# Gate columns of the modulation: both blocks of a tile behind its second half

## The chip, the cores and the metric

The kernel runs on one core of one Trainium2 chip. The metric is the device time of one execution in microseconds (us), taken as the median of several runs. PE is the TensorE engine (matmuls), PEld its weight loads, DVE is VectorE, ACT is ScalarE, POOL is GpSimd, SP is SyncE, whose queue issues the loads.

## What is computed

One step of a hybrid decoder layer for 1024 prompt tokens and 8 sampled sequences of 8 tokens, model width 2048. Cut to what matters here:

```
mod = silu(c) @ w_ada + b_ada            # c: one prompt row and 8 sample rows
shift, scale, gate = split(mod, 3)
xn  = rmsnorm(x, norm_g) * (1 + scale) + shift
z   = xn @ w_in                          # 40 tiles of 128 columns, cut into 8 parts
...                                      # three token mixers: RG-LRU, convolution, spatial gating
out = concat(ya, yb, yc) @ w_out
y   = rmsnorm(x + gate * out, final_g)
```

`shift` and `scale` are needed before `xn`, `gate` only when the out-projection is read out. So the 2048 columns of `w_ada` that give `gate` can be multiplied at any time before that.

## The kernel before

Everything is float32. A large matmul is made of three float32r products: each operand is split into a high and a low part (`split`: a copy on ACT gives the high part, a subtraction on DVE the low part), and `mm3` (L135) adds hi·hi, hi·lo and lo·hi. Those three are the lines L136, L137 and L138 of every table.

The tokens go through in two parts: first 512 prompt tokens (T0), then the other 512 and the 64 sample tokens (T1). The first part begins with the 4096 columns of shift and scale (`ada_block`, tile a_raw), interleaved with six in-projection tiles (`k_step`). Then `IN_SINGLE` lists 34 in-projection tiles of 128 columns, n = 0 to 33, which the loop at L760 does one after the other.

One such tile is `single` (L541). Its weights come in two halves, `h` = 0 and 1, each a load of 512 KB (`w_raw`, three buffers) that is split into two pieces `w_hi`, `w_lo` (five and four buffers). Each half is 8 k-steps of three matmuls, so 24 matmuls of 128x512, all into one PSUM tile `ps_s`. Behind each half `single` calls `extra(h)`.

For the last 16 tiles, n = 18 to 33, `extra` multiplies gate columns. `gate_block` (L156) does one block f of 32: it takes two buffers `g_raw` (the pool tag xr, four buffers), loads 256 KB of `w_ada` into each, and calls `ada_mm` (L147), which issues 8 matmuls of the modulation rows `cz` (32 columns wide, so each fills a quarter of the array's columns) against 128 columns; in the profile a block is 16 matmuls at L151 into `ps_ada`. Eight blocks fill one `ps_ada`; behind the last of them `ada_fin` copies it (ACT, tile rows), transposes it (PE, L174) and adds the bias (DVE, adam).

`ps_s`, `ps_ada` and the out-projection's `ps_g` share three PSUM buffers (pool pmm). While a `ps_ada` is open, the tiles use the other two.

A scheduler sets the order on each engine. It takes the instructions in the order of the program; what stands under `high_priority` (the loads of `w_raw` and `g_raw` and the splits) is taken as if it stood some thousand places earlier, as far as its buffer is free by then. SP issues its loads in that order, and one that waits for its buffer holds up those behind it.

Behind a tile, `part.step()` runs what was deferred by a tile (the gates of the RG-LRU group, `ps_gate`, L440, six pairs of matmuls with 64 rows), and `part.finish` reads the tile out of PSUM, for the RG-LRU tiles with an ACT copy into `pad_a` (L419).

Of the kernel before, what the change touches and what calls it, by code (L numbers as in the profile page):

```python
# [44 lines left out]
def decoder_layer(ctx: ExitStack, tc: tile.TileContext, a):  # L45
# [101 lines left out]
    def ada_mm(pa, b, raw):  # L147
        for q in range(2):
            k = 2 * b + q
            for j in range(4):  # L150
                nc.tensor.matmul(pa[32 * j:32 * j + 32, 0:P], cz[:, k, :], raw[q][:, j * P:(j + 1) * P],  # L151
                                 start=(k == 0), stop=(k == KT - 1))
# [3 lines left out]
    def gate_block(f):  # L156
        u, b = 8 + f // 8, f % 8
        if b == 0:
            gate_ps[u] = pmm.tile([P, 2, 512], F32, tag="mm", name="ps_ada")[:, 0, :]
        raw = []  # L160
        with tc.high_priority(HP):
            for q in range(2):
                r = sp_.tile([P, TM], F32, tag="xr", name="g_raw")
                nc.sync.dma_start(r[:, :512], a["w_ada"][u, b][:, q * 512:(q + 1) * 512])
                raw.append(r)
        ada_mm(gate_ps[u], b, raw)
        if b == 7:
            ada_fin(u, gate_ps[u])

    def ada_fin(u, pa):  # L170
        rows = stp.tile([P, P], F32, tag="rows", name="rows", bufs=1)
        with tc.high_priority(HP):
            nc.scalar.copy(rows, pa[:, 0:P])
        nc.tensor.transpose(pa[:, P:2 * P], rows, ident)  # L174
        with tc.high_priority(HP):
            dst = adam[:, 4 * u:4 * u + 4, :]
            o = VEC["b_ada"][0] + 4 * u
            nc.vector.tensor_tensor(dst, pa[:, P:2 * P].rearrange("p (a b) -> p a b", b=32)[:, :, 0:9],
                                    vec[:, o:o + 4].unsqueeze(2).to_broadcast([P, 4, 9]), op=ALU.add)
            if u < 8:  # L180
                o = VEC["norm_g"][0] + 2 * u
                sc = dst.rearrange("p (a b) n -> p a b n", b=2)[:, :, 1, :]
                nc.vector.scalar_tensor_tensor(
                    sc, sc, 1.0, vec[:, o:o + 2].unsqueeze(2).to_broadcast([P, 2, 9]),
                    op0=ALU.add, op1=ALU.mult)
# [355 lines left out]
    def single(src, xs, T, extra=None):  # L541
        ps = pmm.tile([P, 2, 512], F32, tag="mm", name="ps_s")
        for h in range(2):
            hl = load_w(src[h], 1024, 2)
            for kk in range(8):
                k = h * 8 + kk
                xh, xl = xs(k)
                hi, lo = hl[kk // 4]
                o = kk % 4 * P
                mm_unit(ps, 0, hi[:, o:o + P], lo[:, o:o + P], xh, xl, T,  # L550
                        k == 0, k == KT - 1)
            if extra:
                extra(h)
        return ps
# [205 lines left out]
    for n, ct in enumerate(IN_SINGLE):  # L760
        g0 = (n - 18) * 2
        ps = single(a["wi_s"][n], lambda k: xn[k], T0,
                    (lambda h: gate_block(g0 + h)) if g0 >= 0 else None)
        part.step()
        part.finish(ct, ps, 0)
    part.step(True)
# [119 lines left out]
```

## Time and profile before

| | us |
|---|---|
| median of 3 runs | 1499.89 |
| lowest and highest of these | 1499.72, 1502.18 |
| the profiled execution, its own time | 1500.81 |
| its span, from the first to the last instruction | 1499.1 |
| PE busy in the span | 1457.4 |

The profile is of one execution. The table of all engines says who is busy, the list of waits who stood still and for whom, a timeline shows the starts of the instructions one by one. Matmuls are pipelined: the time one of them takes on the engine is the distance from its start to the next start, not its listed duration, which is longer. A window row gives the busy time of each engine in a stretch, the number of instructions, and the granted TensorE clock as a share of full speed.

### The profile page before, as it was taken

To read this page: it belongs to the slowest core of one execution; us is meant where nothing else is said; L and a number is where in the kernel's file an instruction comes from. 1 tells how busy PE (TensorE), PEld (TensorE's weight loads), DVE (VectorE), ACT (ScalarE), POOL (GpSimd) and SP (SyncE) were. 2 spreads that over 40 slices of the span, in tenths; PEclk is the share of its full clock that TensorE was granted. 3 is DMA by queue.
4 is the path that set the end of the run, shared out by engine and by line. 5 is a ranking of instruction groups with operands and counts; after the bars stand their busy time and mean duration, and the time that the engine had idled before them with its cause. 6 is when DMAs were issued, how large, how long until landed. Compare 5 with 4: busy or idle time off the path is not lost.

```text
span 1499.1 us, 25363 instructions
## 1 busy us (share of the span) xinstructions
PE 1457.4 (97%) x10108; PEld 1304.8 (87%) x10108; DVE 902.0 (60%) x1708; ACT 622.0 (41%) x1042; POOL 49.8 (3%) x120
## 2 busy tenths in 40 slices
PE   4999999999999999999999999999999999999996
PEld 3777888887777778888899999999999999999996
DVE  4436983679467452554895993388956755334345
ACT  4224432274557542443533422236455854223220
POOL 0000000000000000000000100011000000000000
PEclk9999999999999999999999999999999999999998
DMA  9995233324554542564473222222222221244323
GB/s 365 407 361 196 82 102 98 98 91 145 162 162 143 168 152 99 176 196 151 151 246 110 83 86 76 83 85 88 88 87 71 71 89 55 80 130 124 109 79 127
DMA packets 86550, 205.05 MB, mean 137 GB/s; under 512 B 10656, under 2 KB 26656, under 8 KB 86432
## 3 DMA queue, kind: packets, MB, share of 16 engines
q1 hardware_dynamic: 85280, 202.25, 40.8%
q8 instruction: 79, 1.29, 0.3%
q10 hardware_dynamic: 1152, 1.18, 0.2%
q14 instruction: 39, 0.32, 0.1%
HBM read 193.65 MB, written 9.74 MB: 136 GB/s over the span
## 4 chain that ended last, share of the span: by engine, by line
PE 91%; DMA 6%; DVE 2%; issue 0%; ACT 0%; SPq 0%; DVEq 0%; ACTq 0%
PE ps_s L136 24%; PE ps_s L138 23%; PE ps_s L137 23%; PE ps_g L138 5%; PE ps_g L136 5%; PE ps_g L137 5%; DMA a_raw<-w_ada 5%; PE ps_ada L151 2%; PE ps_gate L440 1%; DMA w_raw<-wi_g 1%; DMA x<-x 1%; PE ps_bc L206 1%; PE ps_mix L333 1%; DVE y L643 0%; PE ps_var L215 0%
## 5 line engine op out<-in xcount | busy, mean ns | idle before, releaser
L98 DVE TENSOR_TENSOR w_lo<-w_raw,w_hi 128x512 fp32r<-128x512 f32 (+1 forms) x480 | 311.5, 653 | 408.7 <-PE ps_s L138 264.5
L136 PE MATMUL ps_s<-xn_hi,w_hi 128*128 128x288 f32 (+1 forms) x1632 | 540.6, 331 | 1.8 <-ACT pad_a L419 1.6
L97 ACT CAST w_hi<-w_raw 128x512 fp32r<-128x512 f32 (+1 forms) x480 | 281.1, 591 | 611.4 <-PE ps_s L137 414.7
L137 PE MATMUL ps_s<-xn_lo,w_hi 128*128 128x288 f32 (+1 forms) x1632 | 534.2, 327 | 0.0
L138 PE MATMUL ps_s<-xn_hi,w_lo 128*128 128x288 f32 (+1 forms) x1632 | 532.9, 327 | 0.0
L136 PEld LDWEIGHTS ps_s<-xn_hi,w_hi 128*128 128x128 f32 x1632 | 306.0, 187 | 32.8 <-issue 7.7
L138 PEld LDWEIGHTS ps_s<-xn_hi,w_lo 128*128 128x128 f32 x1632 | 307.1, 188 | 22.3 <-issue 0.3
L137 PEld LDWEIGHTS ps_s<-xn_lo,w_hi 128*128 128x128 f32 x1632 | 306.5, 188 | 21.1 <-issue 1.0
L356 DVE SCALAR_TENSOR_TENSOR mx<-pad_b,vec,mx 128x512 f32<-128x512 f32 x240 | 178.1, 746 | 2.3
L136 PE MATMUL ps_s<-m_hi,w_hi 128*128 128x288 f32 (+1 forms) x480 | 157.1, 327 | 0.0
L137 PE MATMUL ps_s<-m_lo,w_hi 128*128 128x288 f32 (+1 forms) x480 | 156.6, 326 | 0.0
L138 PE MATMUL ps_s<-m_hi,w_lo 128*128 128x288 f32 (+1 forms) x480 | 156.5, 326 | 0.0
L136 PE MATMUL ps_g<-xn_hi,w_hi 128*128 128x288 f32 (+1 forms) x288 | 95.4, 331 | 1.3 <-DVE y L579 0.7
L138 PEld LDWEIGHTS ps_s<-m_hi,w_lo 128*128 128x128 f32 x480 | 90.3, 188 | 6.3
L137 PEld LDWEIGHTS ps_s<-m_lo,w_hi 128*128 128x128 f32 x480 | 90.1, 188 | 6.2
L136 PEld LDWEIGHTS ps_s<-m_hi,w_hi 128*128 128x128 f32 x480 | 90.0, 188 | 6.1
L138 PE MATMUL ps_g<-xn_hi,w_lo 128*128 128x288 f32 (+1 forms) x288 | 93.5, 329 | 1.7 <-DVE w_lo L98 1.7
L136 PE MATMUL ps_g<-m_hi,w_hi 128*128 128x288 f32 (+1 forms) x288 | 94.2, 328 | 0.1
L137 PE MATMUL ps_g<-xn_lo,w_hi 128*128 128x288 f32 (+1 forms) x288 | 94.1, 327 | 0.0
L137 PE MATMUL ps_g<-m_lo,w_hi 128*128 128x288 f32 (+1 forms) x288 | 94.0, 326 | 0.0
L138 PE MATMUL ps_g<-m_hi,w_lo 128*128 128x288 f32 (+1 forms) x288 | 93.6, 326 | 0.0
L138 PEld LDWEIGHTS ps_g<-xn_hi,w_lo 128*128 128x128 f32 x288 | 54.1, 188 | 8.3 <-DVE w_lo L98 4.7
(190 smaller groups left out, 1395.3 us busy)
## 6 DMA issues: line engine op xcount, KB each, us to landing
w_raw<-wi_s SPq DMA_DIRECT2D x136, 512.0 KB, 3.5
w_raw<-wo_s SPq DMA_DIRECT2D x40, 512.0 KB, 3.5
a_raw<-w_ada SPq DMA_DIRECT2D x64, 256.0 KB, 6.7
a_raw<-w_ada SPq DMA_DIRECT2D x32, 512.0 KB, 6.9
g_raw<-w_ada SPq DMA_DIRECT2D x64, 256.0 KB, 2.7
w_raw<-wi_g SPq DMA_DIRECT2D x16, 384.0 KB, 7.2
w_raw<-wo_g SPq DMA_DIRECT2D x16, 384.0 KB, 3.0
w_raw<-wi_g SPq DMA_DIRECT2D x32, 192.0 KB, 2.6
```

Of the source, the lines that this page charges most:

```text
L97: nc.scalar.copy(hi, raw)
L98: nc.vector.tensor_tensor(lo, raw, hi.bitcast(F32), op=ALU.subtract)
L136: nc.tensor.matmul(out, wh, xh, start=start, stop=False)
L137: nc.tensor.matmul(out, wh, xl, start=False, stop=False)
L138: nc.tensor.matmul(out, wl, xh, start=False, stop=stop)
L151: nc.tensor.matmul(pa[32 * j:32 * j + 32, 0:P], cz[:, k, :], raw[q][:, j * P:(j + 1) * P], start=(k == 0), stop=(k == KT - 1))
L206: nc.tensor.matmul(pb[:, c * w:(c + 1) * w], st[0:w, 1, c0 + c:c0 + c + 1].to_broadcast([w, P]), ident[0:w, 0:w], start=True, stop=True)
L333: nc.tensor.matmul(pm[h * 64:h * 64 + 64, c * P:(c + 1) * P], tok[:, c * P + h * 64:c * P + h * 64 + 64], w[:, h * P:(h + 1) * P], start=T ...
L356: nc.vector.scalar_tensor_tensor(out[:, :T0], pad[:, j:j + T0], w[:, j:j + 1], out[:, :T0], op0=ALU.mult, op1=ALU.add)
L440: nc.tensor.matmul(pg[q][:, :n], w[e, 0:P], x[e, u:v], start=first, stop=last)
```

## The change

`extra(0)` does nothing, and `extra(1)` does both blocks of the tile, g0 and g0 + 1, one after the other. The blocks, their loads, their order and the buffers they use stay.

```diff
     for n, ct in enumerate(IN_SINGLE):
         g0 = (n - 18) * 2
         ps = single(a["wi_s"][n], lambda k: xn[k], T0,
-                    (lambda h: gate_block(g0 + h)) if g0 >= 0 else None)
+                    (lambda h: h and (gate_block(g0), gate_block(g0 + 1))) if g0 >= 0 else None)
         part.step()
         part.finish(ct, ps, 0)
```

What it moves is best seen in the built order. On PE, at the end of the tile n = 18 before (xn and w are the operands of the tile, g_raw those of the gate columns; a row with x8 stands for eight equal instructions of the program):

```order
L136 MATMUL ps_s<-xn_hi,w_hi 128x512
L137 MATMUL ps_s<-xn_lo,w_hi 128x512
L138 MATMUL ps_s<-xn_hi,w_lo 128x512
L151 MATMUL ps_ada<-g_raw,cz 32x128 x8
L440 MATMUL ps_gate<-xac_h,s_hi 128x512 x2
```

and in the same place now:

```order
L136 MATMUL ps_s<-xn_hi,w_hi 128x512
L137 MATMUL ps_s<-xn_lo,w_hi 128x512
L138 MATMUL ps_s<-xn_hi,w_lo 128x512
L151 MATMUL ps_ada<-g_raw,cz 32x128 x16
L440 MATMUL ps_gate<-xac_h,s_hi 128x512 x2
```

The eight that stood 24 matmuls earlier, in the middle of the tile, have come to the end, and the tile's 48 matmuls follow each other without a break. This is so in all 16 tiles; the PSUM buffers that the tiles and `ps_ada` get are the same as before.

On SP, the loads around the middle of this stage before (w_raw 3437 and 3483 are the two halves of tile 20, 3559 and 3605 those of tile 21; the g_raw are the two blocks of tile 19 and the first of tile 20):

```order
L104 DMA w_raw_3437<-wi_s 128x1024
L164 DMA g_raw_3359<-w_ada 128x512
L164 DMA g_raw_3361<-w_ada 128x512
L104 DMA w_raw_3483<-wi_s 128x1024
L164 DMA g_raw_3405<-w_ada 128x512
L164 DMA g_raw_3407<-w_ada 128x512
L104 DMA w_raw_3559<-wi_s 128x1024
L129 DMA s_raw_4202<-lruw 128x128
L164 DMA g_raw_3471<-w_ada 128x512
L164 DMA g_raw_3473<-w_ada 128x512
L104 DMA w_raw_3605<-wi_s 128x1024
```

and now (3437 and 3471 are the halves of tile 20, 3559 and 3593 those of tile 21):

```order
L104 DMA w_raw_3437<-wi_s 128x1024
L104 DMA w_raw_3471<-wi_s 128x1024
L164 DMA g_raw_3393<-w_ada 128x512
L164 DMA g_raw_3395<-w_ada 128x512
L164 DMA g_raw_3405<-w_ada 128x512
L164 DMA g_raw_3407<-w_ada 128x512
L104 DMA w_raw_3559<-wi_s 128x1024
L129 DMA s_raw_4202<-lruw 128x128
L104 DMA w_raw_3593<-wi_s 128x1024
L164 DMA g_raw_3505<-w_ada 128x512
L164 DMA g_raw_3507<-w_ada 128x512
```

The four gate loads of a tile now stand together, ahead of both weight halves of the tile two further on, instead of two ahead of each half.

On ACT there is one place where the order of work that PE waits for changes, around the end of tile 25, as a piece of the difference (- before, + now; lb_s belongs to the layer norm of the convolution group, rows to `ada_fin`):

```order
 L405 ACTIVATE lb_s<-mx_1850,vec 128x512
+L97 CAST w_hi<-w_raw 128x512
+L419 COPY pad_a<-ps_s 128x512
 L405 ACTIVATE lb_s<-mx_2606,vec 128x512
-L97 CAST w_hi<-w_raw 128x512
-L419 COPY pad_a<-ps_s 128x512
 L173 COPY rows<-ps_ada 128x128
```

The copy that empties tile 25's PSUM buffer now stands ahead of one of the layer norm's activations, not behind it. Tile 26 uses that same buffer, before and now.

## Rows read from the trace of the kernel before

**Rows 1.** The page: busy time by engine, and the granted clock in 40 slices.

```profile
PE 1457.4 (97%) x10108; PEld 1304.8 (87%) x10108; DVE 902.0 (60%) x1708; ACT 622.0 (41%) x1042; POOL 49.8 (3%) x120
...
PEclk9999999999999999999999999999999999999998
```

**Rows 2.** The page: the chain of work that ended last, by engine.

```profile
PE 91%; DMA 6%; DVE 2%; issue 0%; ACT 0%; SPq 0%; DVEq 0%; ACTq 0%
```

**Rows 3.** Waits of PE, whole span: total us, times, longest us.

```profile
PE ps_g L138 <- DVE w_lo L98: 1.7, 7, 0.2
PE ps_s L136 <- ACT pad_a L419: 1.6, 2, 1.2
```

**Rows 4.** Stretches: us, then busy us (instructions) by engine, PEclk, DMA share, GB/s.

```profile
130.00:345.00 215.00, 214.94 (x1007) 175.34 (x1006) 157.00 (x244) 88.25 (x140) 7.99 (x18) 1.00 0.32 103
345.00:452.00 107.00, 107.00 (x668) 81.28 (x667) 73.34 (x119) 58.92 (x89) 5.30 (x14) 1.00 0.49 155
452.00:560.00 108.00, 107.61 (x692) 81.85 (x691) 61.67 (x97) 63.72 (x99) 3.75 (x10) 1.00 0.48 160
560.00:900.00 340.00, 338.86 (x2056) 306.24 (x2055) 225.81 (x475) 127.06 (x230) 8.51 (x14) 1.00 0.45 143
```

**Rows 5.** PE's timeline around the first gate block: start us, us, instruction.

```profile
350.66 0.39 PE L138 MATMUL ps_s<-xn_hi,w_lo 128*128 128x512 f32 x1
350.98 0.65 PE L151 MATMUL ps_ada<-g_raw,cz 128*32 128x128 f32 x16
351.55 0.50 PE L136 MATMUL ps_s<-xn_hi,w_hi 128*128 128x512 f32 x1
351.89 0.40 PE L137 MATMUL ps_s<-xn_lo,w_hi 128*128 128x512 f32 x1
...
354.45 0.39 PE L136 MATMUL ps_s<-xn_hi,w_hi 128*128 128x512 f32 x1
...
356.94 0.39 PE L138 MATMUL ps_s<-xn_hi,w_lo 128*128 128x512 f32 x1
```

**Rows 6.** Groups of PE's instructions, 345 to 560 us: the gate blocks.

```profile
L151 PE MATMUL ps_ada<-g_raw,cz 128*32 128x128 f32 x512 | 20.6, 279 | 0.0
```

**Rows 7.** PE's timeline: a run of eight modulation blocks at 48 us.

```profile
48.17 0.39 PE L138 MATMUL ps_g<-xn_hi,w_lo 128*128 128x512 f32 x1
48.48 3.70 PE L151 MATMUL ps_ada<-a_raw,cz 128*32 128x128 f32 x128
```

**Rows 8.** PE's timeline at the end of tile 25.

```profile
452.64 0.64 PE L151 MATMUL ps_ada<-g_raw,cz 128*32 128x128 f32 x16
453.68 0.50 PE L136 MATMUL ps_s<-xn_hi,w_hi 128*128 128x512 f32 x1 [0.39 <-ACT pad_a L419]
```

**Rows 9.** ACT's timeline at the same place.

```profile
453.04 0.58 ACT L419 COPY pad_a<-ps_s 128x512 f32<-128x512 f32 x1
```

**Rows 10.** PE's timeline: the middle blocks of tiles 19 and 20.

```profile
364.41 0.64 PE L151 MATMUL ps_ada<-g_raw,cz 128*32 128x128 f32 x16
...
376.97 0.64 PE L151 MATMUL ps_ada<-g_raw,cz 128*32 128x128 f32 x16
```

**Rows 11.** SP's waits, 300 to 560 us: the gate loads.

```profile
SPq L164 <- PE ps_ada L151: 152.5, 30, 8.3
```

**Rows 12.** The gate loads' time from issue to landing.

```profile
DMA to landing us min/median/max: 2.3/2.7/8.4
```

**Rows 13.** PE's timeline at 31 us and 445 us.

```profile
30.77 1.93 PE L151 MATMUL ps_ada<-a_raw,cz 128*32 128x128 f32 x32
32.63 2.08 PE L206 MATMUL ps_bc<-ident,st 128*128 128x128 f32 x8
...
445.33 1.05 PE L206 MATMUL ps_bc<-ident,st 128*128 128x128 f32 x8
```

**Rows 14.** A stretch at 31 us, columns as in rows 4.

```profile
31.00:35.00 4.00, 4.00 (x48) 3.29 (x44) 0.87 (x6) 0.46 (x2) 0.00 (x0) 1.00 1.04 416
```

## The prediction

> **What bounds the kernel now.** Read the table of engines first: PE is busy 97% of the span, no other engine above 60%, and its granted clock stands at full speed (2.4 GHz) in nearly every slice [rows 1]. The chain that ended last is PE's for 91% [rows 2]. Then read the stretches, since an average can hide a stage with another limit. The 16 tiles with gate blocks lie between 345 and 560 us, and there PE is busy 214.6 of 215 us [rows 4]. The list of waits adds that PE's few stops anywhere are of 0.2 to 1.2 us [rows 3]. So the stage is as long as PE's list of work, and what is cut from that list ends the stage earlier. Behind it PE is busy 338.9 of 340 us [rows 4], so an earlier start there is carried on to the end.
>
> Busy does not mean at its peak, though, so the timeline of PE comes last. Away from the gate blocks the 11 matmuls between 354.45 and 356.94 take 2.49 us, 0.226 us each. Around a block the pace is lost in four places [rows 5]: from the last matmul ahead to the block 0.32 us, 0.09 more than the pace; in the block, to the next matmul, 0.57; from that matmul to its successor 0.34, 0.11 too much; and the following 11 steps take 2.56 instead of 2.49, 0.07 too much. Together that is 0.85 us for one visit. As a check, 350.66 to 354.45 is 3.79 us, and its 13 steps would take 2.94 at the pace. The group row has 512 such matmuls, 16 per block, so there are 32 visits [rows 6].
>
> **The change, part by part.** *Visits.* 16 visits in the middle of a tile go, each worth 0.85 us. Their work doesn't: 16 matmuls are added to the visit at the tile's end. What 16 more cost inside a visit isn't in this stage, but the run of 128 at 48 us is the nearest row, since it has the same shapes and also follows dense matmuls at full pace [rows 7]: 3.70 us against 0.65 for 16 [rows 5], so 3.05 for 112, 0.0272 each, 0.44 for 16. From inside a visit (0.65 less one matmul's 0.28 [rows 6], over 15 steps) it would be 0.025 each, 0.40. I take 0.44, as it holds for long runs. The gain is 0.85 - 0.44 = 0.41 us per tile, 6.6 us for 16; with 0.40 it is 0.45 and 7.2. If the slower 11 steps behind a visit grew with its length, 0.07 per tile would be lost again, 1.1 in all: that is the lower bound, 5.5.
>
> *Tile 25.* Here PE waited 0.39 us behind a visit, because tile 26 reuses the buffer that the ACT copy at 453.04 was still emptying [rows 8, 9]. Now the visit ahead of that wait is 0.44 longer, and the copy has one activation fewer ahead of it. The added work therefore falls into the wait: 0.39 more gained, 0 if the copy comes later by as much. I take 0.39, since both changes point the same way.
>
> *Loads.* The same 64 loads are issued, four in a row instead of two and two. They wait for their buffers at the head of SP's queue (30 waits, 152.5 us [rows 11]), so what counts is who stands behind: the weight halves of a tile two further on. All four buffers come free at the end of a tile, and the blocks are due at the end of the next, one tile of 12.56 us later [rows 10]; a load lands in 2.7, at most 8.4 us [rows 12]. The weight half behind them has over a tile to spare, and the second half no longer waits for the middle of a tile. I cost this at nothing; a tile's time covers it, and if a load came later than that, each microsecond would be PE's.
>
> *The middle of the tile.* The visit there gave the third weight piece 0.85 us more to be ready; now it has to be there at once. I cost that at nothing as well: the 18 tiles without gate blocks run in this way, and in their stretch from 130 PE is busy 214.94 of 215 us [rows 4].
>
> The sum is 6.6 + 0.39 = 7.0 us. Against the profiled execution's own 1500.81 us that gives 1493.8; the median of the three runs is 0.92 lower, so 1499.89 - 7.0 = **1492.9**. A measurement of this kernel can tell about 0.2%, 3 us, from no change: the limits are 1496.9 and 1502.9.
>
> **Rivals.** *The visit is paced by its instructions.* At 30.77 us 32 matmuls of the same shape took 1.86 us to the next instruction [rows 13], 0.058 each, and the stretch shows the clock as fully granted [rows 14]. If a visit of 32 went like that here, the second half would cost 16 x 0.058 = 0.93 us instead of 0.44, 0.08 more than the visit saved: 1.3 us slower in all, 1501.2, no change that can be told. For it speaks that this is the only run of exactly 32; against it, that the other instructions there are as slow, and that the run of 128 went at 0.027 [rows 7]. The Trainium skill (TensorE: Matmul & The Clock Gate, "Wait — 56ns, not 53.3ns?") has a mechanism of this kind, a sequencer that spends about 62 ns on each matmul where hardware decode is off; by it 16 matmuls would cost 0.99 us and the time would come to some 1502, as an estimate from that page. By the same section there is otherwise a floor of about 25 ns, and with that the run of 128 agrees at 27.2.
>
> *The slow pace outlasts the visit (slower).* In the same place the eight matmuls behind the 32 took 2.08 us, against 1.05 for the same eight at 445 us [rows 13]. If a longer visit brought PE into that state, each tile would lose 1.86 - (0.57 + 0.44) = 0.85 in the visit and 1.03 behind it, against 0.41 gained: 1.47 us, 23.5 for 16 tiles, 1523. It decides as soon as over 0.41 us per tile comes back. Against it: the run of 128 came from dense matmuls at full pace, as a visit does here, and kept its 0.027 to the end [rows 7], and in this stage PE is busy without a gap [rows 4].
>
> *The cover in the middle was needed.* Where PE did wait for a DVE split elsewhere, it was 1.7 us in 7 waits, 0.24 each [rows 3]. One such wait in each of the 16 tiles takes back 3.9 us: 1496.8. Against it stands the stretch of tiles without a break, above.
>
> **How the numbers follow.** The forecast, 1492.9, has 0.76; its own bounds are 1492.3 (7.2 + 0.39 gained) and 1494.4 (5.5 gained and nothing at tile 25). The needed cover, 1496.8, has 0.09, about half of it on the faster side of the limit. The instruction pace, 1501.2, has 0.10, and the outlasting pace, 1523, has 0.05. That makes faster 0.80, same 0.15, slower 0.05. The range takes in the forecast and the lost cover, with room for the spread of the three runs above the median and, below, for both waits of the kind at tile 25, 1.6 us [rows 3], beside the 7.2: 1491.1 to 1497.5, some 0.83.
>
> **What would show it.** Of the steps, the profile afterwards should show: 16 visits of 32 matmuls at L151, with about 1.08 us listed each, not 0.65 (or 1.93, by the first rival); 48 matmuls of a tile at 0.226 us each without a break; a tile's period shorter by 0.41, some 12.15 us; no wait of PE at tile 25; the stretch of the 16 tiles some 7 us shorter, and everything behind it as long as before. The prediction is wrong if the visit of 32 lists much over 1.1 us, if the steps behind it stay slow for longer than 11, or if PE shows new waits for w_hi, w_lo or g_raw.

## The result and the profile after

The changed kernel takes 1493.44 us, median of 6 runs (1492.29 to 1497.14), beside 1499.81 for the kernel before (1499.37 to 1502.18). The ratio is 0.9949, 95% interval 0.9938 to 0.996: 6.4 us faster, with 1492.9 forecast. The profiled execution took 1494.82 us, 6.0 less than that of before.

The page of after, its span and its table of busy time (engine, busy us, share, number of instructions):

```profile
span 1493.1 us, 25365 instructions
...
PE 1448.9 (97%) x10108; PEld 1305.4 (87%) x10108; DVE 902.3 (60%) x1708; ACT 621.1 (42%) x1042; POOL 52.3 (4%) x120
```

PE has the same 10108 matmuls as in [rows 1] and is busy 8.5 us less with them, while the span is only 6.0 us shorter, so PE stands still 2.5 us longer than before. DVE and ACT are nearly as they were in [rows 1]. Where the two numbers come from is read by stretches. Of after (us, then busy us of PE and its instructions, granted clock, DMA share, GB/s):

```profile
0.00:40.00 40.00, 18.09 (x275) 0.96 0.98 368
...
345.23:549.41 204.18, 204.18 (x1340) 1.00 0.49 159
...
733.30:894.00 160.70, 159.16 (x1233) 1.00 0.44 135
```

and of before, in the same places of the program:

```profile
0.00:40.00 40.00, 19.71 (x276) 1.00 0.97 368
...
345.00:556.07 211.07, 210.68 (x1340) 1.00 0.48 156
...
740.00:900.00 160.00, 159.57 (x1235) 1.00 0.43 136
```

The stage with the gate blocks is 6.89 us shorter, 6.5 of it busy time and 0.39 the wait at tile 25, and the profile lists no wait of PE in it any more. In the first 40 us PE is 1.6 us less busy, but that moves nothing: it stands still for half of that time in either kernel, and the first dense matmul comes at 39.69, at 39.56 before. Around the beginning of the second part, from 733 us, PE waits 1.1 us longer: a part of the gain is given back there.

PE's timeline of after around the end of the second tile with gate blocks (start, listed us, instruction), which answers to [rows 5]:

```profile
369.32 0.39 PE L138 MATMUL ps_s<-xn_hi,w_lo 128*128 128x512 f32 x1
369.64 1.08 PE L151 MATMUL ps_ada<-g_raw,cz 128*32 128x128 f32 x32
370.65 0.50 PE L136 MATMUL ps_s<-xn_hi,w_hi 128*128 128x512 f32 x1
370.99 0.40 PE L137 MATMUL ps_s<-xn_lo,w_hi 128*128 128x512 f32 x1
...
373.50 0.39 PE L136 MATMUL ps_s<-xn_hi,w_hi 128*128 128x512 f32 x1
```

The four places of a visit can be read again. The entry is still 0.32 us. The block is 1.01, which is the 0.57 of before plus the 0.44 forecast for 16 more matmuls. The step behind it is still 0.34. The following 11 steps take 2.51, only 0.02 over the pace, where it was 0.07 before. So two visits became one, and the one is no slower in any place.

The gate blocks of the stage as a group (busy us, mean ns of one, idle before them; compare [rows 6]):

```profile
L151 PE MATMUL ps_ada<-g_raw,cz 128*32 128x128 f32 x512 | 17.3, 276 | 0.0
```

The same 512 matmuls occupy 17.3 us instead of 20.6.

**An account by tile.** For each of the 16 tiles the start of the first dense matmul behind its last visit can be compared between the two traces. After is 0.21 us ahead behind the first of them and 6.66 us ahead behind the last, where the out-projection begins (549.41, before 556.07). It came into the stage 0.23 us late, so the stage gained 6.9 us. Of this 0.61 belongs to tile 25 and 0.42 on average to each of the other fifteen (0.35 to 0.46). A tile without other work beside it takes 12.12 us now, from the visit at 524.17 to that at 536.29, where the period was 12.56 in [rows 10].

### The profile page after: what moved, and what is told of

The parts are those of the page before. It is cut to its first block, busy times and chain, and to the rows that moved or that the text cites. A ratio compares the mean times of both kernels' runs of the same rounds, so it can differ in the third digit from the quotient of the medians.

```text
span 1493.1 us, 25365 instructions
## 1 busy us (share of the span) xinstructions
PE 1448.9 (97%) x10108; PEld 1305.4 (87%) x10108; DVE 902.3 (60%) x1708; ACT 621.1 (42%) x1042; POOL 52.3 (4%) x120
## 4 chain that ended last, share of the span: by engine, by line
PE 91%; DMA 5%; DVE 3%; issue 1%; SPq 0%; ACT 0%; POOL 0%; DVEq 0%; ACTq 0%; POOLq 0%
PE ps_s L136 24%; PE ps_s L138 23%; PE ps_s L137 23%; PE ps_g L138 5%; PE ps_g L136 5%; PE ps_g L137 5%; PE ps_ada L151 2%; DMA a_raw<-w_ada 2%; DMA w_raw<-wi_g 1%; PE ps_gate L440 1%; DMA x<-x 1%; DMA x_n<-x 1%; DVE w_lo L98 1%; PE ps_bc L206 1%; PE ps_mix L333 1%
```

## Experiments

In all of them the stage is taken from the last convolution matmul ahead of it to the first matmul of the out-projection: 384.28 us in before, 377.39 in after. The excess of a visit is the time from the last dense matmul ahead of it to the 13th behind it, less the steps at the pace of 0.226 us: 0.85 for before's visits of 16, 1.24 for after's of 32, each where nothing else stands beside it. If nothing but the number of visits counted, the fixed price of one is twice the first less the second: 2 x 0.85 - 1.24 = 0.46.

The theory was that a visit has a fixed price that goes with the switch from dense 128-column matmuls to 32-column ones and back. The rivals were that the gain comes from the loads or the moved order, that it comes from the place of the visit, and that any interruption of the dense stream costs the same.

**The same kernel again, `after_again`.**

> The changed kernel as it is, beside the others on the same chip. Fixed price of a visit (0.85 us for 16 matmuls against 1.24 for 32 in the two traces, so 0.45 us per visit beside 0.40 us per block): about 1493 us, 6.5 to 7 us under the kernel before. If the 1.1 us that the profiled execution lost around 750 us belongs to the change, the profile shows the wait for the norm's statistics there again with 1.4 us; if it is chance, that wait is near the 0.2 us of before.

Measured: 1494.01 beside 1501.58, ratio 0.9952 [0.994, 0.9965]; the stage 377.28. The stage repeats its gain, 7.0 us. By the medians the whole gains 7.6 us here, where it gained 6.4 in the first measurement. The two differ by as much as the 1.1 us that the first profile lost around 750 us, so that loss can be read from the traces only. The wait for the norm's statistics stands here again, with 1.74 us.

**Both blocks behind the first half, `first_half`.** The same number of visits at the other place (here and in the next diff the line taken out is that of the changed kernel):

```diff
-                    (lambda h: h and (gate_block(g0), gate_block(g0 + 1))) if g0 >= 0 else None)
+                    (lambda h: not h and (gate_block(g0), gate_block(g0 + 1))) if g0 >= 0 else None)
```

> Both blocks of a tile behind its first half instead of its second: as many visits (16 of 32 matmuls), at the other place. If the number of visits is all that counts: 1493, as the change. If the place counts too: in five tiles the visit no longer stands directly ahead of the six gate matmuls, which costs 0.25 us each (in the trace before, a visit alone 0.85 and the gates alone 1.12, together 1.71, not 1.96), 1.2 us in all, and tile 26 waits for its PSUM buffer without a visit as cover, 0.4 to 1 us: 1494.6 to 1495.5. If the gain came from the tile's end alone (the cover of the wait for the buffer, the later opening of the modulation's PSUM buffer), it is gone: 1499.

Measured: 1496.3, ratio 0.9968 [0.9957, 0.998]; the stage 380.48, 3.1 us longer than in after, and a little more than the 1494.6 to 1495.5 that were expected if the place counts. It does. PE's timeline of this kernel shows why: with a visit in the middle of a tile the gate matmuls stand alone at its end (375.70 and 382.38), and a transposition of modulation rows has to wait:

```profile
391.83 0.33 PE L174 MATMUL ps_ada<-ident,rows 128*128 128x128 f32 x1 [0.69 <-ACT rows L173]
```

The visits themselves cost 1.24 as in after. But `ps_gate`, with its 64 rows, breaks the dense stream as well (1.12 by itself), and in five tiles of before and after the visit stands directly ahead of it: together they cost 2.14 in after, not 1.24 + 1.12 = 2.36. Apart, the five tiles lose 0.22 to 0.25 each, 1.1 to 1.25 us. Three new waits add 1.1 (0.69 and 0.17 for rows, 0.23 for a split of the gates' operand). The remaining 0.8 us stand beside these waits: the two transpositions cost about 0.2 each beyond their wait and what one costs elsewhere, and the gate matmuls that waited for their split break the stream in two places instead of one, 1.85 - 0.23 against 1.12, 0.5 more.

**Fewer and longer visits, `four_visit` and `eight_visit`.** Four or eight blocks in one visit, in every second or fourth tile. Since there are only four load buffers, the blocks of a visit share the loads of its first two:

```diff
+    def gate_multi(f0, m):
+        sets = []
+        for f in range(f0, f0 + m):
...
+            if len(sets) < 2:
...
+                sets.append(raw)
+            ada_mm(gate_ps[u], b, sets[f % 2])
...
-                    (lambda h: h and (gate_block(g0), gate_block(g0 + 1))) if g0 >= 0 else None)
+                    (lambda h: h and g0 % 4 == 0 and gate_multi(g0, 4)) if g0 >= 0 else None)
```

> Four blocks in one visit behind every second tile (tiles 18, 20, ... 32): 8 visits of 64 matmuls. Left out: half of the gate loads; the third and fourth block of a visit are multiplied from the buffers of the first two, so half of the gate columns are wrong, with as much work on TensorE. Fixed price per visit: 8 visits fewer than the change at 0.45 us, 3.6 us faster, about 1489.8. If the price grows with the visit's length (a slower pace behind longer visits): 1493. If longer visits fall into the slow pace of the run at 31 us (0.058 us per matmul): 8 visits of 64 cost 3.7 us each instead of 2.0, 1507.

> All eight blocks of a group in one visit behind every fourth tile (18, 22, 26, 30): 4 visits of 128 matmuls. Left out: three quarters of the gate loads, the blocks are multiplied from the buffers of the first two. Fixed price per visit: 12 visits fewer than the change at 0.45 us, 5.4 us, less 0.25 us at two tiles whose gate matmuls then stand alone: about 1488.5. If the price grows with length: 1493.

Measured: `four_visit` 1493.58, ratio 0.9946 [0.9931, 0.9961], stage 375.55; `eight_visit` 1490.99, ratio 0.9931 [0.9918, 0.9945], stage 374.57. PE's timeline of `four_visit` around one visit:

```profile
511.41 0.39 PE L138 MATMUL ps_s<-xn_hi,w_lo 128*128 128x512 f32 x1
511.73 1.95 PE L151 MATMUL ps_ada<-g_raw,cz 128*32 128x128 f32 x64
513.61 0.50 PE L136 MATMUL ps_s<-xn_hi,w_hi 128*128 128x512 f32 x1
513.95 0.40 PE L137 MATMUL ps_s<-xn_lo,w_hi 128*128 128x512 f32 x1
```

Entry and exit are once more 0.32 and 0.34, and the 64 matmuls take 1.88, so 0.87 for 32 more: 0.027 each, as in [rows 7]. The excess is 2.11, the fixed price by it 2 x 1.24 - 2.11 = 0.37. Eight visits fewer should give 3.0 us, and the stage got only 1.8 shorter. Of the rest, 0.6 is two transpositions that now fall between gate matmuls, at 0.47 each instead of 0.16, and 0.28 lies in one tile; 0.3 was not followed. With `eight_visit` it is 1.0 us more for four visits fewer. So merging goes on paying, 0.23 and 0.25 us for each visit saved against 0.43 in the change, and both kernels miss the times expected of a fixed price (1489.8 and 1488.5). `four_visit` came out at the 1493 of the rival that the price grows with the visit's length, but not for its reason: the step behind a visit of 64 and the 11 after it take 0.34 and 2.51, as behind one of 32. Nearly nothing of its gain in the stage reached the whole time, since PE waits 1.62 us at the beginning of the second part (below). A kernel that does the full work in this way needs eight or sixteen load buffers; it wasn't tried.

**More and shorter visits, `quarter`.** The full work, each half block behind a quarter of a tile, 64 visits of 8:

```diff
-            if extra:
-                extra(h)
+                if extra and kk % 4 == 3:
+                    extra(2 * h + kk // 4)
...
-                    (lambda h: gate_block(g0 + h)) if g0 >= 0 else None)
+                    (lambda i: gate_half(g0 + i // 2, i % 2)) if g0 >= 0 else None)
```

> The other direction: half a block (8 matmuls at L151, one load) behind each quarter of a tile, 64 visits instead of 32 of the kernel before, with the same work. Fixed price per visit: 32 more at 0.45 us, 14.4 us slower than before, about 1514. If a visit is paid by its matmuls and not by its breaks: 1500.

Measured: 1512.02 beside 1500.55, ratio 1.0076 [1.0061, 1.0091]; the stage 395.91, 11.6 us longer than before for 32 more visits, 0.36 each. In PE's timeline:

```profile
349.88 0.39 PE L138 MATMUL ps_s<-xn_hi,w_lo 128*128 128x512 f32 x1
350.20 0.42 PE L179 MATMUL ps_ada<-g_raw,cz 128*32 128x128 f32 x8
350.56 0.50 PE L136 MATMUL ps_s<-xn_hi,w_hi 128*128 128x512 f32 x1
350.89 0.39 PE L137 MATMUL ps_s<-xn_lo,w_hi 128*128 128x512 f32 x1
```

The edges are the same again, 0.32 and 0.33, and the eight matmuls take 0.36. The excess is 0.58 to 0.59, so the fixed price is 2 x 0.585 - 0.85 = 0.32. Over all lengths it came out as 0.32, 0.46 and 0.37: a price per visit there is, but by these differences not one constant to better than 0.1 us. They double what is particular to one length. If the work is taken out at 0.0272 a matmul [rows 7] instead, visits of 8, 16, 32 and 64 leave 0.37, 0.41, 0.37 and 0.37: nearly one price, and only the visits of 16 have 0.04 more, in the 11 steps behind them.

**The loads, `half_loads`.** Before's 32 visits, but only every second block is loaded, and the next one multiplies the same data:

```diff
-        raw = []
...
+        if f % 2 == 0:
+            raw = gate_ps["raw"] = []
...
+        ada_mm(gate_ps[u], b, gate_ps["raw"])
```

> The kernel before with its 32 visits, but the second block of a tile multiplied from the buffers of the first: left out is half of the gate loads (8 MB), half of the gate columns are wrong. The control for the kernels that leave loads out. If the loads lie under the tiles, as the prediction costs them: 1499.8, no change. If they or the queue they share with the weights cost PE time: faster by some us, and then as much of the gain of the kernels with fewer loads is theirs.

Measured: 1501.34 beside 1500.55, ratio 1.0 [0.9991, 1.0009]; the stage 384.29 (before 384.28). Half of the gate loads can be left out without a change of the time, so the gain isn't from the loads. The wait behind the last visit of tile 25 stands there too, in PE's timeline of this kernel:

```profile
452.44 0.50 PE L136 MATMUL ps_s<-xn_hi,w_hi 128*128 128x512 f32 x1 [0.39 <-ACT pad_a L420]
```

It is the 0.39 of [rows 8], unchanged, so it isn't the loads that made it either.

**Is any interruption as dear?** Six kernels ask this in pairs. `_split` has before's 32 visits, `_merged` after's 16, and the shape of the gate matmuls is changed in both alike. The difference of a pair is then the price of 16 visits of that shape. First, weights over all 128 columns of the array and 512 columns moved, one matmul for four (`full`):

```diff
-        ada_mm(gate_ps[u], b, raw)
+        for q in range(2):
+            k = 2 * b + q
+            nc.tensor.matmul(gate_ps[u], cz[:, k:k + 4, :].rearrange("p a b -> p (a b)"), raw[q][:, :512],
+                             start=(k == 0), stop=(k == KT - 1))
```

> The kernel before, but a gate block as 2 matmuls over the full 128 columns of the array and 512 wide, instead of 8 over 32 columns and 128 wide. The rows the 9 modulations need are right; what reads them out takes 128 of the 512 columns, so the gate is wrong. More work on TensorE per block (a float32 matmul of this width takes some 0.9 us), so some 40 us slower; only the difference to the merged twin tells. If the fixed price of a visit comes from changing how the array is divided into columns, it is small here: from the lone transpose of 128 columns at 556.9 us, which costs 0.13 to 0.2 us, the visit's excess in the trace is the two matmuls plus 0.2, and merging saves 2 to 3 us. If any break of the run of equal matmuls costs 0.45: merging saves 7.

> The same blocks of 2 full-width matmuls (gate wrong in the same way), both blocks behind the second half as in the change. If the price of a visit is that of dividing the array: 2 to 3 us faster than its split twin. If it is that of any break: 7 us faster.

Measured: `full_split` 1531.97, ratio 1.0205 [1.0191, 1.0219], and `full_merged` 1532.09, ratio 1.0203 [1.0189, 1.0217], beside 1500.55. These matmuls are longer, which is why both lose to before; between the two there is no difference. The stages are 414.88 and 414.20. PE's timeline of `full_split`, and its weight loads (PEld) in the same place:

```profile
366.32 0.39 PE L138 MATMUL ps_s<-xn_hi,w_lo 128*128 128x512 f32 x1
366.55 1.88 PE L168 MATMUL ps_ada<-g_raw,cz 128*128 128x512 f32 x4
367.86 0.79 PE L136 MATMUL ps_s<-xn_hi,w_hi 128*128 128x512 f32 x1
```

```profile
366.10 0.19 PEld L138 LDWEIGHTS ps_s<-xn_hi,w_lo 128*128 128x128 f32 x1
366.32 0.41 PEld L168 LDWEIGHTS ps_ada<-g_raw,cz 128*128 128x128 f32 x2
...
367.83 0.19 PEld L136 LDWEIGHTS ps_s<-xn_hi,w_hi 128*128 128x128 f32 x1 [0.24 <-issue]
```

The block begins 0.23 us behind the matmul ahead of it, at the dense pace, not 0.32; and its first weights are loaded at 366.32, a whole matmul ahead. The excess is 1.78 for a visit and 3.45 for a double one: 2 x 1.78 - 3.45 = 0.11. With these pairs the loads, the order and the place are moved just as in the change, and the time stays. So none of those is the gain.

That still leaves the short matmuls (128 columns moved) as the cause, so the next pair has full-width weights and 128 columns moved (`narrow`), four matmuls where `full` has one:

```diff
+            for j in range(4):
+                nc.tensor.matmul(gate_ps[u][:, j * P:(j + 1) * P], cz[:, k:k + 4, :].rearrange("p a b -> p (a b)"),
+                                 raw[q][:, j * P:(j + 1) * P], start=(k == 0 and j == 0),
+                                 stop=(k == KT - 1 and j == 3))
```

> The kernel before, but a gate block as 8 matmuls over the full 128 columns of the array, still 128 wide each. As with the two full-width twins, what reads the block out takes 128 of the 512 columns, so the gate is wrong. With its merged twin it asks what the price of a visit hangs on: the full-width twins (one matmul 512 wide, all columns of the array) showed 1.78 us for a block alone and 3.45 for two, so a fixed price of 0.11 instead of 0.46. They changed two things, the division of the array and the width. If the division is the price: the excess of one visit here is the work plus 0.1. If the short matmuls are: plus 0.45.

> The same blocks of 8 matmuls over all columns, 128 wide (gate wrong in the same way), both blocks behind the second half. If the price is the division of the array into columns: at most 2 us faster than its split twin, twice one visit's excess less the merged one's is 0.1 us. If it is the short matmuls: 7 us faster, 0.45 us per visit.

Measured, beside 1502.27: 1534.52, ratio 1.022 [1.0205, 1.0235], and 1534.38, ratio 1.0219 [1.0203, 1.0234]. The stages are 416.57 and 416.73, the excess 1.80 and 3.60: a price of 0.00. In PE's timeline of `narrow_split` both edges are smaller, 0.22 into the block and 0.32 behind its first successor:

```profile
365.85 0.39 PE L138 MATMUL ps_s<-xn_hi,w_lo 128*128 128x512 f32 x1
366.07 1.95 PE L169 MATMUL ps_ada<-g_raw,cz 128*128 128x128 f32 x16
367.77 0.48 PE L136 MATMUL ps_s<-xn_hi,w_hi 128*128 128x512 f32 x1
368.09 0.40 PE L137 MATMUL ps_s<-xn_lo,w_hi 128*128 128x512 f32 x1
```

Last the opposite pair, weights of 32 columns with 512 columns moved (`wide32`); the result stands in one quarter, and four copies bring it into the rows:

```diff
+        for q in range(2):
+            k = 2 * b + q
+            nc.tensor.matmul(gate_ps[u][0:32, :], cz[:, k, :], raw[q][:, :512],
+                             start=(k == 0), stop=(k == KT - 1))
...
+                    nc.scalar.copy(rows[32 * j:32 * j + 32, :], pa[0:32, j * P:(j + 1) * P])
```

> The kernel before, but a gate block as 2 matmuls of 32 columns, 512 wide, into the first 32 rows of the buffer, read out by four copies. The array is divided as before, the matmuls are long. If the division is the price of a visit: the excess of a visit of one block, twice, less that of a merged one is 0.35 to 0.45 us. If short matmuls are the price: 0.1 us. The work of a block is that of the full-width twin, about 1.7 us instead of 0.44, so some 40 us slower than before.

> The same blocks of 2 long matmuls of 32 columns, both blocks behind the second half. If the division is the price: 6 to 7 us faster than its split twin. If the short matmuls are: 2 us or less.

Measured, on the same chip as the pair before: 1541.88, ratio 1.027 [1.0254, 1.0285], and 1536.96, ratio 1.0236 [1.0219, 1.0253]. Here merging gains 4.9 us, and 6.05 in the stage (424.69 and 418.64). The excess is 2.11 and 3.78: 0.44 for a visit. PE's timeline of `wide32_split`, and its weight loads:

```profile
366.21 0.39 PE L138 MATMUL ps_s<-xn_hi,w_lo 128*128 128x512 f32 x1
366.53 1.90 PE L168 MATMUL ps_ada<-g_raw,cz 128*32 128x512 f32 x4
```

```profile
365.99 0.19 PEld L138 LDWEIGHTS ps_s<-xn_hi,w_lo 128*128 128x128 f32 x1
366.53 0.14 PEld L168 LDWEIGHTS ps_ada<-g_raw,cz 128*32 128x32 f32 x2 [0.35 <-issue]
```

The entry is 0.32 again, and the first 32-column weights are loaded when their matmul begins, not a matmul ahead. In after it is the same, at the entry and at the exit:

```profile
369.10 0.19 PEld L138 LDWEIGHTS ps_s<-xn_hi,w_lo 128*128 128x128 f32 x1
369.64 0.81 PEld L151 LDWEIGHTS ps_ada<-g_raw,cz 128*32 128x32 f32 x32 [0.35 <-issue]
370.65 0.19 PEld L136 LDWEIGHTS ps_s<-xn_hi,w_hi 128*128 128x128 f32 x1 [0.20 <-issue]
```

The four shapes together, as the price of a visit by the excesses and the shortening of the stage by merging:

| columns of the weights | columns moved | price of a visit, us | stage shorter by, us |
|---|---|---|---|
| 32 (before, after) | 128 | 0.46 | 6.9 |
| 32 (wide32) | 512 | 0.44 | 6.05 |
| 128 (full) | 512 | 0.11 | 0.7 |
| 128 (narrow) | 128 | 0.00 | -0.2 |

The price goes with the 32 columns, whatever is moved through them, and is nearly gone with 128. That PE empties at such a change is argued, not shown: at the entry the first 32-column weights aren't loaded ahead, where full-width ones are. At the exit the rows don't tell the shapes apart, since in `full_split` too the dense weights come only 0.03 us ahead of their matmul (367.83 and 367.86). And the runs don't separate the division of the array from another property of 32-column weights. The Trainium skill (TensorEngine Tiling (Array Packing), "Key Properties") states that a change of the tiling mode drains TensorE. The entry agrees with that, and the runs put 0.32 to 0.46 us on going there and back, 0.44 to 0.46 by the two pairs of this table.

## Why the prediction was right, point by point

*What bounds it: right.* PE's list of work set the length of the stage, and all that was cut from the list ended it earlier. One reading beside it was wrong: PE's stops elsewhere are not all of 0.2 to 1.2 us. The list of waits of before has longer ones than the two lines of [rows 3] (total us, times, longest us):

```profile
PE ps_ada L151 <- DMA a_raw<-w_ada: 19.7, 8, 9.7
...
PE ps_bc L206 <- DVE st L199: 1.8, 2, 1.6
```

They lie outside the stage and touch no term of the sum, but one of the two waits of the second line, 0.22 us long, is the one that grows below.

*Visits: right in mechanism, and nearly in size.* Forecast 0.41 us a tile; the fifteen tiles other than 25 gained 0.42 on average. The parts were 0.85 removed and 0.44 added. The block grew by just 0.44 (0.57 to 1.01). What the forecast didn't have is that the 11 steps behind the longer visit lose 0.02, not 0.07, which makes 0.46 where a visit stands by itself. The lower bound assumed the opposite. With gate matmuls behind the visit 0.43 is added (1.71 for 16, 2.14 for 32), which makes 0.42.

*Tile 25: right in the wait, wrong in the visit.* The forecast was 0.41 + 0.39 = 0.80, and the tile gained 0.61. The 0.39 of the wait was gained as forecast. From the last dense matmul to the next behind the visit it was 1.36 us in before (452.32 to 453.68), 0.47 more than behind the other visits of 16; it is 1.40 in after (448.94 to 450.34), 0.07 more than behind the others of 32. So the 0.44 of added work made this step only 0.04 longer: 0.40 gained, 0.39 forecast. Of the two reasons given only the first holds. ACT's copy and PE's next matmul in after:

```profile
449.71 0.58 ACT L419 COPY pad_a<-ps_s 128x512 f32<-128x512 f32 x1
```

```profile
450.34 0.50 PE L136 MATMUL ps_s<-xn_hi,w_hi 128*128 128x512 f32 x1
```

The copy still starts 0.72 to 0.77 us behind the tile's last dense matmul (453.04 in before, 449.71 now), so the activation that no longer stands ahead of it gained nothing. And it still ends 0.05 us ahead of PE's matmul, in both kernels (453.62 and 453.68 [rows 8, 9], 450.29 and 450.34): it sets that start now as before, but the longer visit covers nearly all of the time until then.

What failed in the sum is the visit. The middle visit of tile 25 wasn't worth 0.85: eight `ps_var` matmuls stood directly ahead of it, which break the dense pace by themselves. In PE's timeline of before

```profile
442.35 0.97 PE L215 MATMUL ps_var<-one_c,ln_s 128*128 128x1 f32 x8
443.25 0.64 PE L151 MATMUL ps_ada<-g_raw,cz 128*32 128x128 f32 x16
443.82 0.50 PE L136 MATMUL ps_s<-xn_hi,w_hi 128*128 128x512 f32 x1
```

it is 1.47 us from `ps_var` to the next dense matmul. In after

```profile
439.61 0.98 PE L215 MATMUL ps_var<-one_c,ln_s 128*128 128x1 f32 x8
440.45 0.49 PE L136 MATMUL ps_s<-xn_hi,w_hi 128*128 128x512 f32 x1
```

it is 0.84: the visit gave 0.63, and less the 0.44 of its work 0.19, where 0.41 was forecast. The row was read tile by tile for the wait, but not for what stood beside the visit. The two terms, a little too small in fifteen tiles and too large in this one, add up to 15 x 0.42 + 0.61 = 6.9, forecast 7.0. That the sum fits better than its terms is luck.

*Loads and the middle of the tile: right.* In `half_loads` the time stays without half of the loads, and the profile of after lists no wait of PE in the stage, so the split weights were ready in the middle of all 16 tiles. The rival of the needed cover falls with that.

*The instruction pace and its outlasting: both fell.* The visits of 32 list 1.08 us, not 1.93, and the steps behind are faster than before, not slower. What the prediction misread is the row on which both rest: it shows TensorE at a lower clock, as far as can be inferred, and not what 32 matmuls cost. Eleven of the fourteen executions list these 32 with 1.93 us, `after_again` and the pairs among them, and in `wide32_split` the clock is on record there (PE's timeline, then the stretch: us, busy us of PE, granted clock, DMA share, GB/s):

```profile
30.96 1.93 PE L151 MATMUL ps_ada<-a_raw,cz 128*32 128x128 f32 x32
```

```profile
31.00:35.00 4.00, 4.00 (x45) 0.50 1.04 411
```

A granted clock of 0.50 is the lower of TensorE's two levels, 1.2 GHz; all 16 tiles of the stage run at the upper one, 2.4 GHz. In before the stretch of [rows 14] prints 1.00, but the trace of before has no record of the clock ahead of 35.2 us: that 1.00 stands for nothing recorded. In after the clock is on record as full from 27.8 to 31.2 us, and the same 32 matmuls of [rows 13], now at 29.61, list 1.17:

```profile
28.63 1.05 PE L215 MATMUL ps_var<-one_d,acc 128*128 128x1 f32 x8
29.61 1.17 PE L151 MATMUL ps_ada<-a_raw,cz 128*32 128x128 f32 x32
```

The eight `ps_var` matmuls ahead of them list 1.05, where they were 1.87 in before; the eight `ps_bc` behind them, at 31.27 and with the clock on record at the lower level, list 2.05, 2.08 in before. That before ran its 32 at the lower level is inferred from the equal durations. The two differences, 0.82 and 0.76, are the 1.6 us by which PE is less busy at the start, and aren't of the change: `after_again` is busy 20.23 us there, before 19.71. Also the 0.0272 of the run of 128 is a mean and no pace of single matmuls: in the trace they start in fours, 0.006 to 0.007 us apart, with some 0.09 to the next four.

*"Everything behind as long as before": wrong, by 1.1 us.* At the beginning of the second part PE waits longer than before. The lines of PE, in before and then in after:

```profile
762.84 1.13 PE L206 MATMUL ps_bc<-ident,st 128*128 128x128 f32 x8 [0.22 <-DVE st L199]
```

```profile
757.12 1.13 PE L206 MATMUL ps_bc<-ident,st 128*128 128x128 f32 x8 [1.35 <-DVE st L199]
```

After was ahead by 6.8 us at 742 and is ahead by 5.7 here. DVE comes later because it waits for the x_n of the norm, a DMA: 2.3 us in three waits of after, the longest in its timeline:

```profile
743.38 0.75 DVE L230 SCALAR_TENSOR_TENSOR x_n<-x_n,adam,rstd 128x512 f32<-128x512 f32 x1 [1.02 <-DMA x_n<-x]
```

In before it was 1.1 us in two waits. One load accounts for the difference, the twelfth of the sixteen of x_n, issued at 745.89 in before and at 739.31 in after, the same 189.8 to 189.9 us behind the end of the stage. The view of the tile x_n for this load alone, in before and then in after:

```profile
DMA to landing us min/median/max: 2.9/2.9/2.9
```

```profile
DMA to landing us min/median/max: 4.0/4.0/4.0
```

`after_again` has the wait too:

```profile
756.64 1.13 PE L206 MATMUL ps_bc<-ident,st 128*128 128x128 f32 x8 [1.74 <-DVE st L199]
```

So have `four_visit` (1.62 us), `eight_visit` (1.70) and `wide32_merged` (1.73); in these five the load takes 3.6 to 4.6 us (in `eight_visit` it is issued 1.9 us later, too). The other nine executions wait 0.22 to 0.39 us, and the load takes 2.8 to 3.2. Among these are `first_half`, whose stage is 3.8 us shorter than before's, and `full_merged` (0.23) and `narrow_merged` (0.24), whose order of loads is that of after. So the order by itself isn't the cause, and neither is a somewhat earlier end of the stage. What makes this load land later stays open. The forecast looked for what is late next within the stage only.

The medians of before and after differ by 6.4 us: 6.9 of the stage, less about 1.1 behind it, would be 5.8, and the rest is within the spread of the runs (1492.29 to 1497.14). That the median lies only 0.5 us from the forecast, which had no such loss, is luck as well. In the profiled executions it is 6.9 less 0.2 ahead of the stage and 1.1 behind it, and 0.4 regained later: 6.0.

## What to carry to other kernels

Where TensorE bounds a stage, look in its timeline at the edges of every small group of matmuls that stands in a dense stream: the price is in the neighbours' steps, not in the group's listed time. Here matmuls with 32-column weights were worth collecting out of a stream with 128 (0.32 to 0.46 us a visit), and worth putting beside others that break the stream anyway; for weights of the full width it made 0.00 to 0.11 us. Before a slow row is taken for a pace, compare the same instructions in other executions, and make sure that the clock is on record there. And before adding a gain up over all places, read each place for what else breaks the stream there, and follow the earlier end to the next load that has to land for it.

## What was not expected of the hardware

In the four shapes tried a visit's price went with the 32-column weights and not with the columns moved: 0.46 and 0.44 us against 0.11 and 0.00 for full-width ones. Two different breaks share a part of their price when they stand side by side: 32-column matmuls followed directly by 64-row ones cost 1.71, apart 0.85 + 1.12 = 1.97. And the same eight `ps_var` matmuls at the start list 1.87 us in most executions and 1.05 in after: TensorE can be at its lower level there, as on record in `wide32_split` (0.50), while a window without a record prints a clock of 1.00.
